# Low halves of the experts' weight slabs in a two-model stack on one core: all subtracted on VectorE instead of one in five on GpSimd

## Chip, cores and metric

One core of one Trainium2 chip (trn2). The metric is the device time of one execution in microseconds (us). All matmuls are on TensorE (PE in the profile), VectorE is DVE, ScalarE is ACT, GpSimd is POOL, and SP issues the loads.

## What is computed

The reference is a stack of two decoder blocks followed by a third one of another kind, on 512 tokens of width 1024. The change touches only the last piece of it, a hierarchical mixture of experts, whose mathematics is this:

```python
def hier_moe(h, w_rg, b_rg, w_re, b_re, w1e, w3e, w2e):
    ...
    flat_idx = g_idx * EXPERTS_PER_GROUP + e_idx
    cw = jnp.sum(jax.nn.one_hot(flat_idx, N_EXPERTS, dtype=f32) * wts[..., None], axis=1)
    ...
    for e in range(N_EXPERTS):
        he = jax.nn.silu(t @ w1e[e]) * (t @ w3e[e])
        out = out + cw[:, e:e + 1] * (he @ w2e[e])
```

There are 32 experts with inner width 256; each token goes to two of them. After the experts come a residual, a norm and the output.

## The kernel before

Everything is in float32 and every large product is made of three matmuls (`mm3`, lines 130 to 134): an operand is split into a high part `h`, rounded to the fp32r format, and a low part `l = x - h`. Line 132 multiplies one operand's high part with the other's low part, L133 the other way round, L134 high with high. A weight slab therefore has to be copied by ACT (the high part) and subtracted by an elementwise engine (the low part) before the three matmuls of its blocks can all run.

The experts run as 16 pairs, expert i together with expert i + 16, in `moe` (L1941). A pair gathers its 128 token rows (`pair_x`, an indirect DMA on GpSimd's queue at L1875), transposes them on PE (L1883), runs eight slabs of w1 and w3 (`pair_h`), transposes the result (`pair_t`, L1912), runs four slabs of w2 (`pair_y`) and scatters the result (`scatter`, L1937, again GpSimd's queue). The stages of successive pairs are overlapped by hand: the gather and transposes of pair i + 2, then `pair_h` of i + 1, then `pair_y` of i.

A slab is 128 x 1024 floats, 512 KB. `eload` (L1829) fetches slabs into a ring of 24 raw buffers, with the loads on SP's queue. `eslab` (L1845) converts the next one. It counts slabs with `self.ns`, and slab number i modulo 5 decides how:

- 0 or 1: `wparts` (L205) makes it in two halves of 512 columns, high part by ACT (L212, tile `wh`), low part by DVE (L213, tile `wl`); four buffers each.
- 2, 3 or 4: one copy of 1024 columns by ACT (L1856, tile `ewh`) and one subtraction of 1024 columns (tile `ewl`), with one buffer for each of the three numbers. For number 2 the subtraction is GpSimd's (L1858), for 3 and 4 DVE's (L1860).

So five converted slabs exist at a time; a slab's buffers come free when PE has used them. The order on each engine is set by the tile framework's scheduler. DVE's other work per pair is two subtractions for the gathered rows (`xgl`, L124), one for the inner result (`el`, L124), two gates (`he`, L1903) and two halves of the weighted output (`ye`, L1932). Those five kinds read one operand from PSUM, or have a single large operand in SBUF; the subtractions of weights read both operands, raw slab and high part, from SBUF.

After the sixteenth pair a branch (L2004) stands on every engine, and the end (residual, last `pair_y`, norm, output) follows.

Of the kernel before, what the change touches and what calls it, by code (L numbers as in the profile page):

```python
# [8 lines left out]
F32 = mybir.dt.float32  # L9
# [30 lines left out]
class Kern:  # L40
# [1804 lines left out]
    def eslab(self, src):  # L1845
        nc = self.nc
        i = self.ns
        self.ns += 1
        if self.split2:
            return self.split2.pop(0)  # L1850
        raw = self.pre.pop(0) if self.pre else self.eload(src)
        i %= 4 if self.tail else 5
        if i < 2:
            return self.wparts(raw, 1024)
        h, l = self.rtile(f"ewh{i}"), self.rtile(f"ewl{i}")
        self.cpy = nc.scalar.activation(h, raw, AF.Copy)  # L1856
        if i == 2:
            nc.gpsimd.tensor_sub(l, raw, h.bitcast(F32))  # L1858
        else:
            self.sub = nc.vector.tensor_sub(l, raw, h.bitcast(F32))  # L1860
        return [(h[:, o:o + 512], l[:, o:o + 512]) for o in (0, 512)]

    def rtile(self, tag):
# [422 lines left out]
```

## Time and profile before

| what | value |
| --- | --- |
| median of 3 runs | 2455.66 us (2454.9 to 2457.92) |
| the profiled execution's own time | 2453.61 us |
| its span in the profile | 2451.8 us |
| PE busy over the span | 96% |
| DVE busy over the span | 71% |
| ACT busy over the span | 50% |
| GpSimd busy over the span | 9%, nearly all of it after 2050 us |
| read from HBM | 320.77 MB |

How to read it: the span is cut by the profile's slices, and shares over the whole span are averages over many stages. The experts fill about 2090 to 2406 us. Matmuls are pipelined, so the time from one matmul's start to the next is what counts, not their durations; the same holds on DVE, where the next instruction starts a little before the one ahead ends.

### The profile page before, as it was taken

To read this page: it belongs to the slowest core of one execution; us is meant where nothing else is said; L and a number is where in the kernel's file an instruction comes from. 1 tells how busy PE (TensorE), PEld (TensorE's weight loads), DVE (VectorE), ACT (ScalarE), POOL (GpSimd) and SP (SyncE) were. 2 spreads that over 40 slices of the span, in tenths; PEclk is the share of its full clock that TensorE was granted. 3 is DMA by queue.
4 is the path that set the end of the run, shared out by engine and by line. 5 is a ranking of instruction groups with operands and counts; after the bars stand their busy time and mean duration, and the time that the engine had idled before them with its cause. 6 is when DMAs were issued, how large, how long until landed. Compare 5 with 4: busy or idle time off the path is not lost. (4 is left out here: it accounts for less than half of the span.)

```text
span 2451.8 us, 37394 instructions
## 1 busy us (share of the span) xinstructions
PE 2357.1 (96%) x14485; PEld 1967.5 (80%) x14485; DVE 1740.6 (71%) x3032; ACT 1221.3 (50%) x2117; POOL 222.8 (9%) x137
## 2 busy tenths in 40 slices
PE   8999999999999999999999999999999997889996
PEld 6887998888888888888888888877778786777775
DVE  6678566676778587666577777775465565899996
ACT  5456454443434455554453434445345434677772
POOL 1000000000000000000000000000000001444544
PEclk9999999999999999999999999899999998899998
DMA  5212342336364421442236363333122065789973
GB/s 171 70 49 70 106 121 61 95 95 193 100 197 141 135 81 50 146 123 67 86 95 201 99 199 100 97 112 121 37 70 61 19 206 207 263 326 353 343 264 115
DMA packets 105419, 333.66 MB, mean 136 GB/s; under 512 B 18736, under 2 KB 18864, under 8 KB 105233
## 3 DMA queue, kind: packets, MB, share of 16 engines
q1 hardware_dynamic: 100768, 322.91, 41.0%
q0 software_dynamic: 4464, 8.27, 1.0%
q8 instruction: 116, 1.90, 0.3%
q14 instruction: 71, 0.57, 0.1%
HBM read 320.77 MB, written 18.35 MB: 138 GB/s over the span
## 5 line engine op out<-in xcount | busy, mean ns | idle before, releaser
L212 ACT ACTIVATE wh<-raw 128x512 fp32r<-128x512 f32 (+1 forms) x660 | 409.9, 625 | 668.1 <-PE pg L134 597.5
L132 PE MATMUL pg<-b,wl 128*128 128x512 f32 (+1 forms) x1808 | 694.6, 385 | 0.7 <-ACT b L126 0.7
L133 PE MATMUL pg<-b,wh 128*128 128x512 f32 (+1 forms) x1808 | 691.3, 383 | 1.4 <-DVE b L127 1.4
L134 PE MATMUL pg<-b,wh 128*128 128x512 f32 (+1 forms) x1808 | 691.1, 383 | 0.0
L213 DVE TENSOR_TENSOR wl<-raw,wh 128x512 fp32r<-128x512 f32 (+1 forms) x660 | 460.1, 701 | 187.6 <-ACT wh L212 182.4
L132 PEld LDWEIGHTS pg<-b,wl 128*128 128x128 f32 x1808 | 340.9, 189 | 66.9 <-ACT b L126 0.9
L133 PEld LDWEIGHTS pg<-b,wh 128*128 128x128 f32 x1808 | 341.2, 189 | 66.4 <-DVE b L127 1.6
L134 PEld LDWEIGHTS pg<-b,wh 128*128 128x128 f32 x1808 | 341.0, 189 | 65.5
L133 PE MATMUL pg<-hx,wh 128*128 128x512 f32 x384 | 157.1, 409 | 2.2 <-issue 1.4
L132 PE MATMUL pg<-hx,wl 128*128 128x512 f32 x384 | 153.6, 404 | 2.6 <-ACT hx L123 2.6
L134 PE MATMUL pg<-hx,wh 128*128 128x512 f32 x384 | 155.2, 404 | 0.0
L345 DVE TENSOR_TENSOR t<-pg,b 128x512 f32<-128x512 f32 x118 | 81.5, 691 | 89.7 <-PE pg L134 89.4
L296 POOL TENSOR_TENSOR rt<-v,mhalf 128x4 f32<-128x4 f32 (+2 forms) x12 | 17.4, 1452 | 1181.7 <-DVE v L294 1091.0
L213 DVE TENSOR_TENSOR wl<-eraw,wh 128x512 fp32r<-128x512 f32 x132 | 113.8, 910 | 3.1 <-ACT wh L212 3.1
L1856 ACT ACTIVATE ewh<-eraw 128x1024 fp32r<-128x1024 f32 x92 | 97.3, 1060 | 31.8 <-PE pg L134 18.0
L133 PE MATMUL pg<-wl,b 128*128 128x256 f32 x384 | 109.0, 284 | 2.5 <-DVE wl L213 2.3
L132 PE MATMUL pg<-wh,b 128*128 128x256 f32 x384 | 109.0, 284 | 0.4 <-DVE b L127 0.4
L134 PE MATMUL pg<-wh,b 128*128 128x256 f32 x384 | 108.7, 283 | 0.0
L350 DVE TENSOR_TENSOR x<-x,pg 128x512 f32<-128x512 f32 x80 | 54.9, 686 | 65.9 <-PE pg L134 65.4
L1858 POOL TENSOR_TENSOR ewl<-eraw,ewh 128x1024 fp32r<-128x1024 f32 x32 | 91.2, 2849 | 98.8 <-ACT ewh L1856 98.6
L1860 DVE TENSOR_TENSOR ewl<-eraw,ewh 128x1024 fp32r<-128x1024 f32 x60 | 88.5, 1499 | 2.8 <-ACT ewh L1856 2.8
L212 ACT ACTIVATE wh<-eraw 128x512 fp32r<-128x512 f32 x132 | 79.3, 626 | 21.8 <-PE pg L134 14.5
(668 smaller groups left out, 4156.3 us busy)
## 6 DMA issues: line engine op xcount, KB each, us to landing
eraw<-in_w_dram SPq DMA_DIRECT2D x98, 512.0 KB, 5.8
raw<-in_ffn_up_dram SPq DMA_DIRECT2D x88, 512.0 KB, 3.7
mraw<-in_w_mod_dram SPq DMA_DIRECT2D x64, 512.0 KB, 4.5
eraw<-in_w2e_dram SPq DMA_DIRECT2D x60, 512.0 KB, 6.2
raw<-in_w_in_dram SPq DMA_DIRECT2D x36, 512.0 KB, 3.7
raw<-in_ffn_down_dram SPq DMA_DIRECT2D x32, 448.0 KB, 3.4
raw<-in_w_dram SPq DMA_DIRECT2D x28, 512.0 KB, 5.2
raw<-in_w_attn_qk_dram SPq DMA_DIRECT2D x16, 512.0 KB, 3.6
```

What stands on the lines that cost most here:

```text
L132: nc.tensor.matmul(ps, ll, rh, start=start, stop=False)
L133: nc.tensor.matmul(ps, lh, rl, start=False, stop=False)
L134: nc.tensor.matmul(ps, lh, rh, start=False, stop=stop)
L212: self.cpy = nc.scalar.activation(h[:, :m], raw[:, o:o + m], AF.Copy)
L213: self.sub = nc.vector.tensor_sub(l[:, :m], raw[:, o:o + m], h[:, :m].bitcast(F32))
L296: nc.gpsimd.tensor_tensor(r[:, :w], v[:, :w], self.mhalf[:, :w], op=OP.pow)
L345: self.nc.vector.tensor_mul(t[0:p], ps[0:p, :], self.rb[0:p])
L350: self.nc.vector.tensor_add(xb[i], xb[i], ps)
L1856: self.cpy = nc.scalar.activation(h, raw, AF.Copy)
L1858: nc.gpsimd.tensor_sub(l, raw, h.bitcast(F32))
L1860: self.sub = nc.vector.tensor_sub(l, raw, h.bitcast(F32))
```

## The change

The branch for slab number 2 is removed, so that numbers 2, 3 and 4 are all subtracted by DVE. Nothing else is edited; the lines below move up by three (L1860 becomes L1857, L1903 becomes L1900, L1932 becomes L1929, L1937 becomes L1934, L1875 becomes L1872).

```diff
         h, l = self.rtile(f"ewh{i}"), self.rtile(f"ewl{i}")
         self.cpy = nc.scalar.activation(h, raw, AF.Copy)
-        if i == 2:
-            nc.gpsimd.tensor_sub(l, raw, h.bitcast(F32))
-        else:
-            self.sub = nc.vector.tensor_sub(l, raw, h.bitcast(F32))
+        self.sub = nc.vector.tensor_sub(l, raw, h.bitcast(F32))
         return [(h[:, o:o + 512], l[:, o:o + 512]) for o in (0, 512)]
```

The scheduler puts the moved subtractions into DVE's queue. On DVE, in the middle of the experts, about one pair (a number behind a tile's name is its buffer's; 22891, 22903 are the low parts of slabs 3 and 4 of one round, 22879 that of slab 2). Before:

```order
L124 TENSOR_TENSOR xgl_22799<-pa,xgh_22798 128x512 x2
L1860 TENSOR_TENSOR ewl_22891<-eraw,ewh_22890 128x1024
L1860 TENSOR_TENSOR ewl_22903<-eraw,ewh_22902 128x1024
L213 TENSOR_TENSOR wl<-eraw,wh 128x512 x2
L1903 SCALAR_TENSOR_TENSOR he<-s_22872,mk,pg 128x256
L213 TENSOR_TENSOR wl<-eraw,wh 128x512 x2
L1860 TENSOR_TENSOR ewl_22964<-eraw,ewh_22963 128x1024
L1860 TENSOR_TENSOR ewl_22976<-eraw,ewh_22975 128x1024
L1903 SCALAR_TENSOR_TENSOR he<-s_22928,mk,pg 128x256
```

The same place now:

```order
L124 TENSOR_TENSOR xgl_22799<-pa,xgh_22798 128x512 x2
L213 TENSOR_TENSOR wl<-eraw,wh 128x512 x4
L1857 TENSOR_TENSOR ewl_22879<-eraw,ewh_22878 128x1024
L1857 TENSOR_TENSOR ewl_22891<-eraw,ewh_22890 128x1024
L1900 SCALAR_TENSOR_TENSOR he<-s_22872,mk,pg 128x256
L1857 TENSOR_TENSOR ewl_22903<-eraw,ewh_22902 128x1024
L213 TENSOR_TENSOR wl<-eraw,wh 128x512 x4
L1857 TENSOR_TENSOR ewl_22952<-eraw,ewh_22951 128x1024
L1900 SCALAR_TENSOR_TENSOR he<-s_22928,mk,pg 128x256
L1857 TENSOR_TENSOR ewl_22964<-eraw,ewh_22963 128x1024
L1857 TENSOR_TENSOR ewl_22976<-eraw,ewh_22975 128x1024
```

One subtraction more stands in each round of five slabs (22879, 22952), ahead of those of slabs 3 and 4, and the gates `he` have moved by one or two places.

On GpSimd's queue, in the third to sixth pair (yd is the scatter, xg the gather). Before:

```order
L1858 TENSOR_TENSOR ewl_20882<-eraw,ewh_20881 128x1024
L1858 TENSOR_TENSOR ewl_20976<-raw,ewh_20975 128x1024
L1937 DMA yd<-ye,ids 1024x1024
L1875 DMA xg_20588<-h2d,ids 128x1024
L1858 TENSOR_TENSOR ewl_21046<-eraw,ewh_21045 128x1024
L1858 TENSOR_TENSOR ewl_21155<-eraw,ewh_21154 128x1024
L1937 DMA yd<-ye,ids 1024x1024
L1875 DMA xg_20589<-h2d,ids 128x1024
L1858 TENSOR_TENSOR ewl_21227<-eraw,ewh_21226 128x1024
```

Now:

```order
L1934 DMA yd<-ye,ids 1024x1024
L1872 DMA xg_20588<-h2d,ids 128x1024
L1934 DMA yd<-ye,ids 1024x1024 x2
L1872 DMA xg_20589<-h2d,ids 128x1024
L1872 DMA xg_20588<-h2d,ids 128x1024
L1934 DMA yd<-ye,ids 1024x1024 x2
```

Only gathers and scatters are left there in the experts, and some neighbours among them have changed places.

## Rows read from the trace of the kernel before

**Rows 1.** The page: the span, and each engine's busy time.

```profile
span 2451.8 us, 37394 instructions
PE 2357.1 (96%) x14485; PEld 1967.5 (80%) x14485; DVE 1740.6 (71%) x3032; ACT 1221.3 (50%) x2117; POOL 222.8 (9%) x137
```

**Rows 2.** Busy time of each engine by stretch; from 2110, cuts are starts of L1912.

```profile
core 0: us, PE busy (x) PEld busy (x) DVE busy (x) ACT busy (x) POOL busy (x), PEclk, DMA share, GB/s
...
2020.00:2035.00 15.00, 15.00 (x80) 12.63 (x79) 5.39 (x10) 5.38 (x11) 0.00 (x0) 1.00 1.03 410
2110.00:2129.50 19.50, 19.50 (x101) 16.59 (x100) 18.48 (x23) 16.56 (x25) 8.24 (x4) 1.00 0.80 270
2129.50:2147.20 17.70, 17.70 (x86) 14.79 (x85) 17.16 (x20) 15.29 (x23) 9.76 (x5) 1.00 0.99 366
2147.20:2384.70 237.50, 220.44 (x1009) 178.31 (x1008) 234.89 (x257) 181.03 (x262) 115.22 (x51) 0.99 0.89 329
2384.70:2405.60 20.90, 18.64 (x77) 14.99 (x76) 16.62 (x20) 9.69 (x14) 7.83 (x12) 0.92 0.08 32
```

**Rows 3.** Instructions in order of time, PE, 2110 to 2130: start us, us, instructions.

```profile
2122.26 1.95 PE L1529 MATMUL pa<-ident,mod 128*128 128x128 f32 x16
```

**Rows 4.** Who waited for whom, PE, 2110 to 2406: us in total, times, longest.

```profile
PE pg L133 <- DVE wl L213: 15.5, 10, 2.8
PE pa L133 <- DVE wl L213: 2.3, 1, 2.3
```

**Rows 5.** Groups by line and shape, 2110 to 2385, DVE and GpSimd: busy us, mean ns.

```profile
L213 DVE TENSOR_TENSOR wl<-eraw,wh 128x512 fp32r<-128x512 f32 x115 | 100.2, 921 | 0.0
L1860 DVE TENSOR_TENSOR ewl<-eraw,ewh 128x1024 fp32r<-128x1024 f32 x52 | 78.9, 1543 | 2.4 <-ACT ewh L1856 2.3
...
L1932 DVE SCALAR_TENSOR_TENSOR ye<-pa,wsl,row 128x512 f32<-128x512 f32 x26 | 18.2, 738 | 1.0 <-PE pa L134 1.0
L124 DVE TENSOR_TENSOR xgl<-pa,xgh 128x512 fp32r<-128x512 f32 x28 | 17.9, 675 | 0.0
...
L1858 POOL TENSOR_TENSOR ewl<-eraw,ewh 128x1024 fp32r<-128x1024 f32 x28 | 81.5, 2910 | 86.6 <-ACT ewh L1856 86.4
```

**Rows 6.** Instructions in order of time, 2150 to 2172: DVE, GpSimd, one of PE.

```profile
2152.07 4.67 DVE L213 TENSOR_TENSOR wl<-eraw,wh 128x512 fp32r<-128x512 f32 x3
...
2159.32 2.48 DVE L213 TENSOR_TENSOR wl<-eraw,wh 128x512 fp32r<-128x512 f32 x4
2161.73 1.21 DVE L1860 TENSOR_TENSOR ewl<-eraw,ewh 128x1024 fp32r<-128x1024 f32 x1
2162.86 0.46 DVE L1903 SCALAR_TENSOR_TENSOR he<-s,mk,pg 128x256 f32<-128x256 f32 x1
2163.26 3.04 DVE L1860 TENSOR_TENSOR ewl<-eraw,ewh 128x1024 fp32r<-128x1024 f32 x1
...
2152.59 2.38 POOL L1858 TENSOR_TENSOR ewl<-eraw,ewh 128x1024 fp32r<-128x1024 f32 x1
2160.29 4.93 POOL L1858 TENSOR_TENSOR ewl<-eraw,ewh 128x1024 fp32r<-128x1024 f32 x1 [5.31 <-ACT ewh L1856]
...
2155.58 0.50 PE L133 MATMUL pg<-wl,xgh 128*128 128x512 f32 x1 [1.89 <-DVE wl L213]
```

**Rows 7.** Instructions in order of time, DVE, near 2386 us.

```profile
2386.79 1.40 DVE L1932 SCALAR_TENSOR_TENSOR ye<-pa,wsl,row 128x512 f32<-128x512 f32 x2
2388.11 1.21 DVE L1860 TENSOR_TENSOR ewl<-eraw,ewh 128x1024 fp32r<-128x1024 f32 x1
...
2389.84 5.09 DVE L213 TENSOR_TENSOR wl<-eraw,wh 128x512 fp32r<-128x512 f32 x4
```

**Rows 8.** Instructions in order of time, DVE, where the experts begin.

```profile
2095.84 1.43 DVE L124 TENSOR_TENSOR xgl<-pa,xgh 128x512 fp32r<-128x512 f32 x2 [3.40 <-ACT xgh L123]
```

**Rows 9.** Who waited for whom, 2110 to 2406, GpSimd and DVE.

```profile
POOL ewl L1858 <- ACT ewh L1856: 109.9, 27, 7.6
...
DVE ewl L1860 <- ACT ewh L1856: 2.3, 3, 1.4
```

## Prediction

> **What bounds the kernel now.** The change can only act in the experts, so I read the page first for the whole and then cut the span. Over the span PE is the busy engine and DVE has room, 71% [rows 1]; that average says nothing about the experts. The busy times by stretch do [rows 2]. The cuts from 2110 us are starts of the transposes L1912, one per pair: 2110 to 2384.7 holds 14 pairs. The second of them took 17.70 us with PE busy throughout, and the first 19.50, also with PE busy throughout, because it holds the making of a row, 1.95 us [rows 3]. So PE's own need is 17.7 us a pair, and 14 pairs would take 14 x 17.7 + 1.8 (19.50 - 17.70) = 249.6 us. They took 274.7. In the twelve pairs from 2147.2 on (19.8 us each) PE is busy 220.44 of 237.5 us and DVE 234.89: **there DVE is the bound, not PE**. The waits say the same: PE stood for DVE's `wl` eleven times, 17.8 us together [rows 4], and where PE stops and starts a little more is lost.
>
> Why is DVE full? Its weight subtractions are longer than the work in them. The mean of `wl` is 921 ns and of DVE's `ewl` 1543 [rows 5], but undisturbed four `wl` start within 2.41 us (2159.32 to 2161.73), 0.60 each, and an `ewl` hands over after 1.13 us (2161.73 to 2162.86) [rows 6]. The long ones lie beside GpSimd's subtraction: three `wl` took 4.67 us from 2152.07 where 1.8 are due, while GpSimd subtracted from 2152.59 for 2.38 us; PE's next L133 then stood 1.89 us. It also goes the other way: the GpSimd one at 2160.29 took 4.93 us, twice its own length, and the `ewl` at 2163.26 took 3.04 until that one was through [rows 6]. Two subtractions with both inputs in SBUF do not run side by side; one holds the other. `xgl` and `ye`, with one input in PSUM, keep 675 and 738 ns [rows 5].
>
> The Trainium skill says this of the port: in SBUF — State Buffer, section Who interferes with whom, a DVE instruction with two SBUF inputs contends with a GpSimd instruction that reads SBUF, and the later one waits for the whole of the other. The trace agrees, with 4.67 us for three `wl`.
>
> **The change, part by part.** A pair has 12 slabs, and of every five one moves, so 2.4 a pair, 33.6 in the 14 pairs.
>
> *Added to DVE:* 33.6 x 1.13 = 38.0 us of work.
>
> *DVE's need afterwards,* per pair: 4.8 slabs in halves, 9.6 x 0.60 = 5.76; 7.2 whole ones x 1.13 = 8.14; `xgl` twice and `el` once, with the length of an undisturbed `wl`, 3 x 0.60 = 1.80; two `he` at 0.40 (2162.86 to 2163.26) [rows 6], 0.80; two `ye`, 1.32 together (2386.79 to 2388.11) [rows 7]. Sum 17.8 us, for 14 pairs 249.5.
>
> *Removed from DVE:* what it loses to GpSimd. Before, its work without the moved ones was 249.5 - 38.0 = 211.5 us, but it was busy 18.48 + 17.16 + 234.89 = 270.5 [rows 2]. The difference, 59.0 us, is the holding, 1.76 us for each GpSimd subtraction. So GpSimd's share costs DVE 59 us to save it 38: DVE's busy time should fall by 21 us in this stretch.
>
> *What the stretch then takes.* PE needs 249.6 us and DVE 249.5: both become equal bounds, so neither can hide the other's waits. DVE was idle 4.2 us of 274.7 when it was alone the bound. With two equal engines and only five converted slabs between them I take 7 us over the larger need, half a microsecond a pair; ends: 0 (PE never waits, as in the second pair) and 14 (1 us a pair, about what its other work, 3.9 us a pair in bursts, could cost). The stretch: 249.6 + 7 = 257, a gain of **18** us (11 to 25).
>
> *From 2384.7 to 2405.6:* PE is busy 18.64 of 20.90 us at a granted clock of 0.92 [rows 2]; one wait of 2.3 us stands here [rows 4], behind four `wl` that took 5.09 us where 2.4 are due [rows 7]. Two of the moved subtractions lie here, 2.3 us of DVE, which was busy only 16.62. I take a gain of **3** us (1 to 4). What follows, the branch and the end, starts when PE is through and moves up unchanged.
>
> *Before 2110:* two moved subtractions. The first stands with the other `ewl` of its round ahead of `xgl`, for which DVE stood idle 3.40 us [rows 8]: it takes 1.13 of that, cost 0. If that cover were gone it would cost 1.1. The second is of the same kind; 0.
>
> *ACT, SP, GpSimd's queue.* ACT's copies are unchanged and it is busy 181 of 237.5 us [rows 2]. Loads must come faster: 14 pairs moved 270 x 19.5 + 366 x 17.7 + 329 x 237.5 = 89.9 MB, in 257 us that is 350 GB/s; 410 were moved from 2020 to 2035 and 366 in the second pair [rows 2]. So no price. On GpSimd's queue scatters and gathers stand without subtractions between them; the swapped neighbours wait for the same point of a pair, and nobody waits for them soon. Cost 0; if a gather came late, PE would stand at the transposes L1883, where no wait is listed now.
>
> Sum: 18 + 3 = **21 us less**. Against the profiled execution's own 2453.6 us that is 2432.6; the median of the three runs is 2.0 us above that execution, which gives 2434.7. I put **2434 us**.
>
> **Rivals.**
>
> *PE at its floor* (the ends at 25 and 4 us): 29 less, 2424.6 to 2426.7, say 2426. For it: the second pair ran without a stop although DVE lost time to GpSimd in it. Against: DVE would have to be busy over 99% without making PE wait.
>
> *DVE's queue holds itself up.* GpSimd waited 109.9 us for ACT's copies, 27 times [rows 9], and this hurt nobody. The moved subtraction waits in DVE's queue with all behind it. If the two engines lose 1 us a pair by that, the gain is 11 + 1 = 12, 2442 to 2444. If it is 1.8 us a pair (25 us), nothing is left, 2454. Against: DVE itself waited for those copies 2.3 us, three times [rows 9]; a full DVE comes late to a copy.
>
> *The holding stays.* Then DVE is a saturated engine that gets 38.0 us of work back: 270.5 + 38.0 = 308.5 us in the stretch, 34 us more, **2488 us**. It decides if the long subtractions come from something else that runs in the same moments, such as the loads or the copies; the change turns from gain to loss where the holding falls below 38.0 / 33.6 = 1.13 us for a moved subtraction that goes away. Against: the long ones stand exactly under GpSimd's, and the short ones at 2159.32 run beside loads and copies as well [rows 6]. The Trainium skill holds both sides: Perfetto Trace Analysis, section Optimizing Scalar/DVE Operations, says that with DVE saturated, giving work to ScalarE or even GpSimd may make sense, which speaks against this change and by the rows would be these 2488; it adds that the two share a read port so that moving work between them might not help, and the 1.76 us above side with that.
>
> **How the numbers follow.** Forecast, 2429 to 2439: 0.54. PE at its floor, 2426: 0.15. Gain halved, 2443: 0.21. Nothing left, within 0.2% (4.9 us, about what a measurement of this kernel can tell from no change): 0.06. Slower, 2488: 0.04. Faster is 0.54 + 0.15 + 0.21 = 0.90. The range 2426 to 2445 takes in the floor and the halved gain and leaves out the last two and some of the ends.
>
> **What would show it.** Right: undisturbed `wl` near 680 ns and `ewl` near 1210 in the mean, DVE's busy time from first to fifteenth L1912 near 250 us, that stretch near 257 us, PE's waits for `wl` below 8 us, GpSimd without TENSOR_TENSOR there. Wrong: `wl` still above 800 ns in the mean (the holding has another source); DVE idle for ACT's copies by more than 10 us; PE standing at L1883 for a gather; or loads that land later than their slab is wanted.

## The result, and the profile after

The changed kernel takes 2430.66 us (median of 4 runs, 2428.38 to 2431.14), the one before, measured with it, 2455.28 (4 runs, 2451.44 to 2457.92): ratio 0.9896, 95% interval 0.988 to 0.9912, **24.6 us less**. A second measurement (run r1 below) gave 2430.57 and 0.9899 (0.9883 to 0.9916). The profiled execution took 2430.2 us.

The page of the changed kernel, its span and engines (before: [rows 1]):

```profile
span 2428.4 us, 37460 instructions
PE 2350.2 (97%) x14485; PEld 1963.5 (81%) x14485; DVE 1721.5 (71%) x3070; ACT 1218.0 (50%) x2117; POOL 107.3 (4%) x99
```

DVE took over 38 subtractions (x3070 instead of x3032) and is busy 19.1 us less. The busy times by stretch show where. Cuts are starts of the transposes L1909 (L1912 before). The lines are one pair, four pairs, nine pairs, the time from the fifteenth transpose until PE is through ahead of the branch, and last the 14 pairs together (before: [rows 2]):

```profile
core 0: us, PE busy (x) PEld busy (x) DVE busy (x) ACT busy (x) POOL busy (x), PEclk, DMA share, GB/s
2110.40:2129.80 19.40, 19.40 (x101) 16.55 (x100) 17.99 (x26) 16.46 (x25) 1.04 (x1) 1.00 0.85 288
2129.80:2200.70 70.90, 70.90 (x338) 59.06 (x337) 70.18 (x93) 59.58 (x88) 8.86 (x8) 1.00 0.98 364
2200.70:2365.00 164.30, 162.52 (x758) 131.79 (x757) 161.55 (x216) 134.09 (x196) 17.70 (x16) 1.00 0.94 355
2365.00:2385.80 20.80, 20.80 (x109) 17.41 (x107) 17.79 (x23) 12.04 (x19) 3.20 (x10) 1.00 0.19 60
2110.40:2365.00 254.60, 252.82 (x1194) 207.41 (x1193) 249.72 (x333) 210.13 (x309) 27.60 (x25) 1.00 0.94 352
```

The 14 pairs took 274.7 us and take 254.6, 20.1 less. Four pairs run at 17.7 us with PE busy throughout; the last nine take 18.3 each, and there DVE is busy 161.55 of 164.30 us. From the fifteenth L1909 to the end it was 67.1 us (2384.7 to 2451.8) and is 63.4, 3.7 less; the experts begin 0.4 us later. 20.1 + 3.7 - 0.4 = 23.4 us, which is the difference of the two spans. The medians differ by 1.2 us more than these two profiled executions.

Groups by line and shape, DVE, from 2105 to 2375 (before: [rows 5]):

```profile
L1857 DVE TENSOR_TENSOR ewl<-eraw,ewh 128x1024 fp32r<-128x1024 f32 x88 | 103.7, 1219 | 1.6 <-ACT ewh L1856 1.6
L213 DVE TENSOR_TENSOR wl<-eraw,wh 128x512 fp32r<-128x512 f32 x120 | 75.9, 685 | 0.0
L1929 DVE SCALAR_TENSOR_TENSOR ye<-pa,wsl,row 128x512 f32<-128x512 f32 x28 | 19.7, 745 | 0.5 <-PE pa L134 0.5
L124 DVE TENSOR_TENSOR xgl<-pa,xgh 128x512 fp32r<-128x512 f32 x28 | 18.0, 682 | 0.0
```

The subtractions of weights went from 921 and 1543 ns in the mean to 685 and 1219. `ye` and `xgl`, with an input in PSUM, were not lengthened before either (738 and 675 in the mean). In order of time the same piece of work as in [rows 6] now reads, on DVE:

```profile
2150.74 2.49 DVE L213 TENSOR_TENSOR wl<-eraw,wh 128x512 fp32r<-128x512 f32 x4
2153.14 2.35 DVE L1857 TENSOR_TENSOR ewl<-eraw,ewh 128x1024 fp32r<-128x1024 f32 x2
2155.41 0.48 DVE L1900 SCALAR_TENSOR_TENSOR he<-s,mk,pg 128x256 f32<-128x256 f32 x1
2155.80 1.22 DVE L1857 TENSOR_TENSOR ewl<-eraw,ewh 128x1024 fp32r<-128x1024 f32 x1
2156.94 2.49 DVE L213 TENSOR_TENSOR wl<-eraw,wh 128x512 fp32r<-128x512 f32 x4
```

Every round is now 2.4 us for four `wl`, and three `ewl` at 1.13 each. Who waits for whom, PE, 2105 to 2395 (before: [rows 4]):

```profile
PE pa L1909 <- DVEq L2001: 5.7, 1, 5.7
PE pg L133 <- DVE wl L213: 0.7, 2, 0.4
PE pg L133 <- DVE ewl L1857: 0.7, 3, 0.4
```

The 17.8 us for `wl` are 0.7; the 5.7 us are PE's wait at the branch, which was 4.3 before. On GpSimd's queue, in the 14 pairs, nothing but gathers and scatters is left, and their long waits hold nobody:

```profile
POOL yd L1934 <- DVE ye L1929: 128.0, 8, 18.3
POOL xg L1872 <- PE pa L1880: 90.8, 6, 16.8
```

### The profile page after: what moved, and what is told of

It reads as the page before. It is cut to its first block, busy times and chain, and to the rows that moved or that the text cites. A ratio compares the mean times of both kernels' runs of the same rounds, so it can differ in the third digit from the quotient of the medians.

```text
span 2428.4 us, 37460 instructions
## 1 busy us (share of the span) xinstructions
PE 2350.2 (97%) x14485; PEld 1963.5 (81%) x14485; DVE 1721.5 (71%) x3070; ACT 1218.0 (50%) x2117; POOL 107.3 (4%) x99
## 4 chain that ended last, share of the span: by engine, by line
PE 68%; issue 23%; DVE 4%; DMA 2%; ACT 1%; POOL 1%; SPq 0%; POOLq 0%; DVEq 0%; ACTq 0%
PE pg L132 18%; PE pg L133 18%; PE pg L134 18%; PE pa L133 2%; PE pa L132 2%; PE pa L134 2%; PE pa L496 1%; PE pa L1213 1%; DMA mraw<-in_w_mod_dram 1%; PE pa L304 1%; DVE t L124 0%; PE pa L1238 0%; PE pa L290 0%; PE pa L1242 0%; DMA yk<-yd 0%
## 5 line engine op out<-in xcount | busy, mean ns | idle before, releaser
L213 DVE TENSOR_TENSOR wl<-raw,wh 128x512 fp32r<-128x512 f32 (+1 forms) x660 | 448.1, 683 | 183.0 <-ACT wh L212 179.7
L1857 DVE TENSOR_TENSOR ewl<-eraw,ewh 128x1024 fp32r<-128x1024 f32 x92 | 108.4, 1219 | 1.6 <-ACT ewh L1856 1.6
L960 DVE SCALAR_TENSOR_TENSOR mraw<-mraw,cb 128x1024 f32<-128x1024 f32 x64 | 77.9, 1222 | 14.4 <-DMA mraw<-in_w_mod_dram 14.2
L133 PEld LDWEIGHTS pg<-hx,wh 128*128 128x128 f32 x384 | 73.1, 190 | 18.3 <-issue 2.0
L132 PEld LDWEIGHTS pg<-hx,wl 128*128 128x128 f32 x384 | 73.3, 191 | 17.1 <-ACT hx L123 3.1
L213 DVE TENSOR_TENSOR wl<-eraw,wh 128x512 fp32r<-128x512 f32 x132 | 83.9, 686 | 3.9 <-ACT wh L212 3.8
```

Source lines behind the costliest of these rows:

```text
L132: nc.tensor.matmul(ps, ll, rh, start=start, stop=False)
L133: nc.tensor.matmul(ps, lh, rl, start=False, stop=False)
L213: self.sub = nc.vector.tensor_sub(l[:, :m], raw[:, o:o + m], h[:, :m].bitcast(F32))
L960: nc.vector.scalar_tensor_tensor(raw, raw, 1.0, cb, op0=OP.mult, op1=OP.mult, accum_out=self.mod_acc[:, j:j + 1])
```

## The experiments

The theory: GpSimd's subtraction, by reading SBUF, holds DVE's two-input instructions for longer (1.76 us) than it spares DVE (1.13). Rivals: the long instructions come from something else in the same moments; what was won comes from GpSimd's queue being empty; PE, not DVE, is what remains. All ratios below are to the kernel before, measured beside each run.

**1. More of it.** GpSimd subtracts two slabs in five (against the kernel before):

```diff
-        if i == 2:
+        if i == 2 or i == 3:
             nc.gpsimd.tensor_sub(l, raw, h.bitcast(F32))
```

> GpSimd subtracts slabs 2 and 3 of every five instead of none. Theory (holding: each GpSimd subtraction costs DVE 1.76 us and saves it 1.13): DVE's need in the 14 pairs is 249.5 - 76 + 67 x 1.76 = 291 us, the stretch 295 us, the time about 2475 us (2463 to 2490), slower than with one in five; mean wl above 1100 ns. Rival (a saturated DVE is helped by giving work away, the kernel with one in five was slow only because GpSimd's result comes late): DVE need 174 us, PE waits for GpSimd's ewl instead of wl; if those waits double from the 1.5 us of before, the time stays near 2455 us.

Measured: 2501.74 us (2 runs, 2498.5 to 2505.0), ratio 1.0186 (1.0135 to 1.0236). From first to fifteenth transpose, busy times:

```profile
2111.30:2435.80 324.50, 276.60 (x1194) 219.17 (x1193) 292.66 (x268) 214.48 (x309) 206.48 (x93) 0.94 0.79 277
```

DVE's busy time is as expected. It executes 268 instructions where the changed kernel has 333, so 249.7 - 65 x 1.13 = 176.3 us of it is its own work, and the holding is 116.4 us, **1.79 us** for each of the 65 that DVE no longer does, or 1.71 for each of the 68 that GpSimd made in this stretch: nearly the same price as with half as many. `wl` took 1167 ns in the mean, as forecast. The time is outside the range all the same, because DVE was not full: it was idle 31.8 us. Its waits in this stretch:

```profile
DVE ewl L1860 <- ACT ewh L1856: 14.6, 11, 2.9
DVE he L1903 <- ACT s L1902: 9.3, 6, 4.1
DVE ye L1932 <- PE pa L134: 7.2, 6, 2.9
```

They are in the main waits for work that itself waits for DVE or GpSimd: ACT's copies `ewh` stood 36.8 us for PE, PE stood 46.9 us for low parts (five rows of its waits), and PE's granted clock was 0.94 in the mean, so that part of the stretch ran at the lower of its two levels, 1.2 GHz. How much of the lateness is the clock's and how much the ring's was not separated.

**2. The holding alone.** The changed kernel, and GpSimd subtracts a raw slab from itself once DVE is done with it. Nobody reads the result.

```diff
         self.sub = nc.vector.tensor_sub(l, raw, h.bitcast(F32))
+        if i == 2 and not self.tail:
+            nc.gpsimd.tensor_sub(raw, raw, raw)
```

> The changed kernel, and besides GpSimd subtracts the raw slab 2 of each round from itself after DVE has used it; nobody reads the result, so nothing can wait for GpSimd's lateness except the raw buffer's release, which has 20 slabs of lead. Theory (holding): DVE's busy time in the 14 pairs 250 + 33.6 x 1.76 = 309 us, the stretch about 311, the time about 2488 us (2472 to 2508), slower than both kernels. Rival (what was lost before was the lateness of GpSimd's result, or the order the scheduler made for it): 2431 us, as the changed kernel, DVE's mean wl near 685 ns.

Measured: 2468.55 us (8 runs, 2462.4 to 2471.6), ratio 1.0051 (1.0039 to 1.0062): work that nothing needs makes the changed kernel 38 us slower, slower than the kernel before. The 14 pairs:

```profile
2105.10:2395.80 290.70, 263.48 (x1194) 206.35 (x1193) 290.10 (x333) 211.89 (x309) 138.40 (x58) 0.99 0.84 310
```

DVE executes the same 333 instructions as in the changed kernel and is busy 40.4 us longer (290.10 against 249.72), 1.22 us for each of the 33 idle subtractions. It is less than the 1.76 that was expected, and the time is below the range. In order of time, GpSimd, then DVE beside it:

```profile
2161.76 1.89 POOL L1859 TENSOR_TENSOR eraw<-eraw 128x1024 f32<-128x1024 f32 x1 [4.71 <-DVE ewl L1857]
...
2161.60 0.47 DVE L1902 SCALAR_TENSOR_TENSOR he<-s,mk,pg 128x256 f32<-128x256 f32 x1
2161.99 3.87 DVE L1857 TENSOR_TENSOR ewl<-eraw,ewh 128x1024 fp32r<-128x1024 f32 x2
```

The idle one is through after 1.89 us where the real one took 2.38 [rows 6], and DVE's two `ewl` end 1.5 us later than the 2.35 of the changed kernel. The two `ewl` end 2.21 us after GpSimd is through (2163.65 and 2165.86), about the length of two of them, as if both had waited for it. So a shorter instruction holds for a shorter time; the expectation took the price of the real one.

**3 to 5. Which part of it holds?** Three more idle works in the same place (the condition line is that of experiment 2): a copy with one SBUF input, a write with none, and two inputs in the copy's two pieces.

```diff
+            for o in (0, 512):
+                nc.gpsimd.tensor_copy(raw[:, o:o + 512], raw[:, 512 - o:1024 - o])
```

> As the one before, but GpSimd copies within the raw slab (two copies of 512 columns: one input from SBUF, not two). Theory (any GpSimd read of SBUF holds DVE's two-input subtraction for its whole length): slower than the changed kernel by 33.6 times most of the two copies' length; with 0.5 to 1 us a copy that is 25 to 60 us, 2455 to 2490 us. Rival (only two inputs on both sides collide): 2431 us and wl near 685 ns.

```diff
+            nc.gpsimd.memset(raw, 0.0)
```

> As the two before, but GpSimd only writes: a memset of the raw slab after its use. Theory (it is GpSimd's reading that holds DVE): 2431 us (2427 to 2435), wl and ewl near 685 and 1220 ns in the mean also beside a memset. Rival (any GpSimd instruction on SBUF holds DVE, or its writes do): the memset's length, some 0.9 us, 33.6 times: about 30 us, 2460 us.

```diff
+            for o in (0, 512):
+                nc.gpsimd.tensor_sub(raw[:, o:o + 512], raw[:, o:o + 512], raw[:, 512 - o:1024 - o])
```

> Idle GpSimd work as with the copies, in the same two pieces of 512 columns per slab, but with two SBUF inputs (a subtraction of one half of the raw slab from the other, which nobody reads). If what held DVE less in the copies is that they have one input: the pieces hold like the whole idle subtraction, DVE busy near 285 to 290 us from first to fifteenth transpose of the inner result, 2463 to 2470 us. Rival, what held less is that the pieces are short: DVE busy near 261 us, 2434 to 2438 us as with the copies.

| idle work of GpSimd | shortest of its kind, us | time, us | ratio to before | DVE busy in the 14 pairs, us | more than 249.72, a piece |
| --- | --- | --- | --- | --- | --- |
| 33 subtractions of 1024 | 1.89 | 2468.55 | 1.0051 (1.0039 to 1.0062) | 290.10 | 1.22 |
| 66 subtractions of 512 | 1.29 | 2471.29 | 1.0071 (1.0054 to 1.0087) | 298.63 | 0.74 |
| 66 copies of 512 | 0.61 | 2435.71 | 0.9907 (0.988 to 0.9933) | 261.15 | 0.17 |
| 33 writes of 1024 | 0.95 | 2428.82 | 0.9889 (0.9848 to 0.9929) | 249.84 | 0.00 |

The writes came out as the theory said. The copies cost far less than it said (2455 to 2490 us), and the pieces of a subtraction somewhat more (2463 to 2470).

The busy times of the stretch with the pieces of a subtraction:

```profile
2107.20:2405.90 298.70, 270.87 (x1193) 204.08 (x1192) 298.63 (x333) 213.71 (x309) 182.28 (x91) 0.99 0.83 302
```

with the copies:

```profile
2111.30:2373.20 261.90, 256.60 (x1193) 206.00 (x1192) 261.15 (x332) 210.52 (x309) 126.20 (x91) 1.00 0.91 343
```

and with the writes:

```profile
2110.30:2365.10 254.80, 253.07 (x1194) 207.47 (x1193) 249.84 (x333) 210.20 (x309) 59.91 (x58) 1.00 0.95 352
```

The write kept GpSimd busy at the same points of the program and cost DVE nothing, so what holds is neither GpSimd's activity nor its queue but its reading. Short pieces alone do not make the holding small either: pieces of 512 with two inputs cost DVE more than four times as much as copies of the same size. But a copy is also the shorter instruction. The shortest, median and longest of each kind in ns, for the copies, the pieces, the whole idle subtraction and the real one before:

```profile
L1860 POOL COPY eraw<-eraw x64: 608/1487/4407, 2093.9 to 2392.2; 128x512 f32<-128x512 f32 x64
L1860 POOL TENSOR_TENSOR eraw<-eraw x64: 1292/2150/5080, 2091.4 to 2429.2; 128x512 f32<-128x512 f32 x64
L1859 POOL TENSOR_TENSOR eraw<-eraw x32: 1888/2756/5681, 2089.0 to 2414.5; 128x1024 f32<-128x1024 f32 x32
L1858 POOL TENSOR_TENSOR ewl<-eraw,ewh x32: 2353/2572/4930, 2092.2 to 2400.2; 128x1024 fp32r<-128x1024 f32 x32
```

If the shortest is the undisturbed length, the price is that length less 0.4 to 0.7 us for all four kinds: 0.17 for 0.61, 0.74 for 1.29, 1.22 for 1.89 and 1.76 for 2.35. So the length of a reading instruction can account for the prices. Whether its second input costs anything beyond making it longer was not separated; a one-input instruction as long as a subtraction was not tried. In order of time, GpSimd and DVE with the copies:

```profile
2162.59 2.17 POOL L1860 COPY eraw<-eraw 128x512 f32<-128x512 f32 x2 [3.54 <-DVE ewl L1857]
...
2158.49 2.90 DVE L213 TENSOR_TENSOR wl<-eraw,wh 128x512 fp32r<-128x512 f32 x4
2161.32 1.21 DVE L1857 TENSOR_TENSOR ewl<-eraw,ewh 128x1024 fp32r<-128x1024 f32 x1
2162.46 0.47 DVE L1903 SCALAR_TENSOR_TENSOR he<-s,mk,pg 128x256 f32<-128x256 f32 x1
2162.85 2.99 DVE L1857 TENSOR_TENSOR ewl<-eraw,ewh 128x1024 fp32r<-128x1024 f32 x2
```

and with the pieces of a subtraction:

```profile
2165.06 3.53 POOL L1860 TENSOR_TENSOR eraw<-eraw 128x512 f32<-128x512 f32 x2 [3.57 <-DVE ewl L1857]
...
2165.30 4.37 DVE L1857 TENSOR_TENSOR ewl<-eraw,ewh 128x1024 fp32r<-128x1024 f32 x2
```

Two copies make two `ewl` 0.64 us longer (2.99 against 2.35), two pieces of a subtraction 2.02. In both cases the last `ewl` ends 1.08 us after GpSimd is through (2164.76 and 2165.84; 2168.59 and 2169.67), about its own length, as if it had begun only then. The Trainium skill, SBUF — State Buffer, section Who interferes with whom, excludes GpSimd instructions that only write, and the writes agree, with 0.1 us for 33 of them. It calls the port shared by DVE and GpSimd an exclusive lock and makes no difference between one and two inputs of a GpSimd instruction that reads; the rows just shown agree with it, for the copies as for the pieces.

**6. What is left above PE's own need.** The changed kernel, but slab 0 of a round gets no low part; its high part stands in for it in the matmul:

```diff
+        if i == 0 and not self.tail:
+            hs = [self.wp.tile([128, 512], F32R, name="wh", tag="wh", bufs=4) for _ in range(2)]
+            for h, o in zip(hs, (0, 512)):
+                self.cpy = nc.scalar.activation(h, raw[:, o:o + 512], AF.Copy)
+            return [(h, h) for h in hs]
```

> The changed kernel, but slab 0 of each round gets no low part at all (its high part stands in for it in the matmul; that part of the computation is left out): DVE is relieved of two wl in five slabs, 2.9 us a pair, with PE's work unchanged. Theory (after the change DVE and PE are equal bounds and what is above PE's floor of 249.6 us is DVE's): the 14 pairs take 249.6 to 250.5 us instead of 254.6, DVE idle above 35 us there, the time 2424 to 2427 us. Rival (what is left above the floor comes from PE itself, from ACT's copies or the loads): 254 us and 2430 us.

Measured: 2425.5 us (2424.6 to 2428.3), ratio 0.989 (0.9868 to 0.9913). The 14 pairs:

```profile
2109.80:2359.10 249.30, 249.30 (x1194) 208.72 (x1193) 218.04 (x267) 210.11 (x309) 33.17 (x25) 1.00 0.95 360
```

PE does not stop at all, at loads that come faster still (360 GB/s). So 249.3 us is PE's need, and the 5.3 us that the changed kernel takes above it are DVE's.

**7 to 9. The same holding elsewhere.** GpSimd also works beside DVE ahead of the experts (additions `th`, L1680) and in the end (additions of `yk`, products with the gain). Experiment 7 gives the end's work to DVE, 8 the rows `th`, 9 both. The cores of the edits:

```diff
-                nc.gpsimd.tensor_add(a, a, y1)
+                nc.vector.tensor_add(a, a, y1)
...
-                    nc.scalar.activation(u, self.xt[2 * t + half], AF.Copy, scale=r[:, t:t + 1])
-                    nc.gpsimd.tensor_add(u, u, self.srow[half])
+                nc.vector.scalar_tensor_tensor(u, self.xt[2 * t + half], r[:, t:t + 1], self.srow[half],
+                                               op0=OP.mult, op1=OP.add)
```

> The changed kernel with the same thing done at the end: the three additions of two halves and the products with the gain, GpSimd's until now, all on DVE. Theory (GpSimd's two-input work holds DVE's there too: subtractions of 3.40 us for 1.2, PE's wait of 1.12 us for the last one, two products of 128 columns in 3.39 us): the last subtractions take 1.2 us each, PE's wait goes, and the end comes 2 to 4 us earlier, about 2428 us. Rival (DVE's chain at the end is serial and full, what GpSimd did beside it now stands in it: 3 additions of 1.1 us and 3.3 us of products): 2431 to 2434 us, not faster.

> The changed kernel with the rows before the experts (scaled by ACT, shift added by GpSimd, seven of eight) all made by DVE, one instruction each. In the routing DVE's chain of small instructions is what the gather waits for, and GpSimd's additions stand beside it: a comparison of 16 columns took 1.23 us there. Theory (each of those additions holds the chain by up to 1 us, five such in the trace): the chain loses about 5 us of holding and gets 7 x 0.6 = 4.2 us of work: between 3 us faster and 2 us slower, 2428 to 2432 us, with the small comparisons near 0.2 us. Rival (those long ones have another reason, such as the end of the instruction ahead): they stay near 1 us and the time is 2434 us or more.

> The changed kernel itself once more, so that the two versions of this call are compared with it on the same chip. Both theories: 2430 us (2427 to 2432), as before.

> The end's additions and gain products and the rows ahead of the experts all go to DVE (the two edits tried apart before). Theory that GpSimd's two-input work held DVE there too: the profile gives 0.6 us ahead of the experts and 2.2 us in the end, so 2427 us (2425 to 2429), some 3 us under the changed kernel. Rival, the edits only move the wait to DVE's own queue: 2430 to 2432, no difference from the changed kernel.

Measured: 2431.64 us (6 runs, 2429.9 to 2437.0; ratio 0.991, 0.9893 to 0.9927) for the end, 2427.71 (6 runs, 2423.8 to 2431.6; 0.9894, 0.9876 to 0.9912) for the rows, and 2427.41 (4 runs, 2425.4 to 2431.1; 0.9894, 0.9877 to 0.991) for both, and 2430.57 (4 runs, 2428.0 to 2431.0) for the changed kernel. Only the last two were measured beside each other. For the end that is the time of the rival (2431 to 2434), for the rows it is just below the theory's range, for both within it. The holding is plain in the traces. In order of time, the changed kernel, GpSimd and DVE ahead of the experts and in the end:

```profile
2069.46 7.89 POOL L1680 TENSOR_TENSOR th<-th,srow 128x512 f32<-128x512 f32 x6 [0.83 <-ACT th L1679]
...
2072.44 1.23 DVE L1700 TENSOR_TENSOR arena<-iot,arena 128x16 f32<-128x16 f32 x1
...
2392.45 9.02 POOL L2094 TENSOR_TENSOR yk<-yk 128x1024 f32<-128x1024 f32 x3
...
2395.82 3.40 DVE L1988 TENSOR_TENSOR lastl<-last,xgh 128x1024 fp32r<-128x1024 f32 x1
```

The comparison of 16 columns with the rows on DVE:

```profile
2076.74 0.16 DVE L1696 TENSOR_TENSOR arena<-iot,arena 128x16 f32<-128x16 f32 x1
```

and `lastl` with both on DVE:

```profile
2391.88 1.22 DVE L1984 TENSOR_TENSOR lastl<-last,xgh 128x1024 fp32r<-128x1024 f32 x1
```

What it is worth is small. From the last L1514 (the `x` ahead of the routing) to the end of the span the changed kernel takes 366.0 and 365.7 us in its two profiles; with the end on DVE 363.8, with the rows 365.6, with both 362.6. So the end on DVE does give some 2 us in its profile; that execution was the slowest of its six (2437.02) because it was late before that point (last L1514 at 2071.4 us against 2062.4 and 2063.6). With both, the gather comes 24.1 us after L1514 instead of 25.0 to 25.3, and the tail from the fifteenth transpose takes 62.85 us instead of 63.3 to 63.4 (with the end alone it took 61.25; why the two differ was not found); the rest lies between the gather and the first transpose (20.9 us against 22.7), and why it is shorter there was not found. The median with both is 3.2 us lower than that of the changed kernel, as the theory had it, but the ranges of the runs overlap: that it beats the changed kernel is not shown.

## Why the prediction was right

It said 2434 us (2426 to 2445); the time is 2430.66. By its steps:

- **DVE, not PE, was the bound of the pairs, and its need would be 249.5 us.** It is busy 249.72. PE's need of 249.6 us is 249.3 in experiment 6.
- **The holding costs 59.0 us, 1.76 a subtraction.** DVE's busy time fell by 20.8 us (270.5 to 249.7) with 33 instructions more in it (300 to 333); 21 was predicted. Experiment 1 gives 1.71 to 1.79, and experiment 2 shows the cause by itself. One row was read loosely: the `ewl` at 2163.26 [rows 6] ended 1.08 us after GpSimd's subtraction was through (2166.30 and 2165.22), about its own length, and not together with it.
- **The stretch, gain 18 us: 20.1.** The term that was mis-sized is the 7 us over the larger need. It is 5.0 (254.6 - 249.6): the last nine pairs make it up (164.3 us against 9 x 17.7 = 159.3), and the first five add nothing. In those nine DVE was busy 161.55 us, 2.3 more than PE's need, and idle for 2.75: it was the bound there. I had spread half a microsecond over every pair. Why the first five ran without a stop was not tested; in four of them DVE executed 93 instructions, 23.3 a pair, and in the last nine 216, 24.0 a pair.
- **The tail, gain 3 us: 3.7.** PE's work from the fifteenth transpose to the branch took 24.7 us (2384.7 to 2409.4, where its last rows L1529 end) and takes 20.8, without a stop at a granted clock of 1.00 (2.4 GHz): 3.9 us for the 3 that were taken. The wait of 2.3 [rows 4] is gone, and with it a stretch at the lower clock: before, the eight matmuls from the one that waited on started 0.43 us apart in the mean (2393.27 to 2396.74) where 0.23 is usual, 1.7 us more; the granted clock from 2392 to 2397 was 0.66. That the rest "moves up unchanged" is right only in the sum, which is luck: the branch's transposes come 1.4 us later after PE is through (5.68 us against 4.33), and the end from them on is 1.2 us shorter (36.9 against 38.1). In the end, the 24 transposes L2043 behind the branch took 3.80 us instead of 5.63, at a granted clock of 0.74 instead of 0.54, and a wait of PE of 1.12 us for `lastl` is new. Why the branch came later was not found.
- **Before 2110, 0:** 0.4 us later, less than two profiles of the changed kernel differ there (2110.4 and 2111.3).
- **Loads, ACT, GpSimd's queue, 0.** The loads ran at 352 GB/s (350 was worked out); PE waited for no gather, though gathers and scatters stood 219 us in their queue.

Of the rivals, *PE at its floor* is out by 5.3 us, which experiment 6 shows to be DVE's. *DVE's queue holds itself up* did not come: in the 14 pairs DVE waited once for an ACT copy of 1024 columns, for 1.1 us. *The holding stays* (2488 us) is refuted by the result, in which the subtractions are down to 685 and 1219 ns, and by experiment 2, where GpSimd's subtraction alone brings the long ones back. The Trainium skill, Perfetto Trace Analysis, section Optimizing Scalar/DVE Operations, says that a saturated DVE may give work to GpSimd, with the caveat that the shared port might keep it from helping. The caveat is what the runs bear out, and they go beyond it: the work given away did not merely fail to help, it cost 24.6 us.

What was less well understood is the size of the holding for other instructions. I carried 1.76 us over to an idle subtraction (1.22), for a copy I took most of a length of 0.5 to 1 us (0.17), and for experiment 1 I took little more than DVE's need, which held for its busy time and missed the 32 us of its idling.

## What to carry to other kernels

Before an elementwise step goes to GpSimd to relieve VectorE, compare what VectorE would need for it (here 1.13 us) with how much longer VectorE's own two-input instructions get beside it (here 1.76 us): a group's mean length beside its undisturbed length (here 921 against 685 ns, 1543 against 1219) shows the holding. VectorE's busy time includes it, so a full VectorE can be busy for less time after taking work back. If GpSimd has to work beside it, writes cost VectorE nothing here, and each of the four kinds of reading instruction cost its own shortest length less 0.4 to 0.7 us.

## What the runs showed of the hardware that was not expected

- A GpSimd copy of 512 columns (0.61 us at the shortest) made DVE's work 0.17 us longer in the mean, a subtraction of the same size (1.29 us) 0.74, and a write of 1024 columns (0.95 us) 0.00.
- The holding does not go by the size of DVE's instruction: a comparison of 16 columns took 1.23 us beside GpSimd's additions and 0.16 without them.
- With GpSimd at two slabs in five, PE's granted clock fell to 0.94 in the mean of the 14 pairs (1.00 after the change), while PE stood 46.9 us for low parts.
